# A Winograd-style 3x3 convolution on one core: a fourth image pair loaded in fp32, later casting loads in halves, fixed output buffers

## The chip, the core and the metric

The kernel runs on one core of a Trainium2 chip. The metric is the device time of one execution in microseconds (us). The core has the engines PE (matrix multiply, TensorE), PEld (its weight loads), DVE (VectorE), ACT (ScalarE), POOL (GpSimd) and SP (SyncE, which here only issues transfers). Transfers between the main memory and the on-chip memory run on 16 DMA engines. Three engines issue them, each through a queue of its own: SP (q1 in the profile), ACT (q10) and POOL (q0). Only POOL's transfers change the data type on the way ("casting loads").

## The reference

`x` is 16 images of 64 channels by 64 x 64 (fp32), `weight` is 128 x 64 x 3 x 3, and the output is 16 x 128 x 64 x 64 in fp32:

```
x_pad = np.pad(x, ((0, 0), (0, 0), (1, 1), (1, 1)))
output[b, co] += weight[co, ci, kh, kw] * x_pad[b, ci, kh:kh+h, kw:kw+w]
```

## The kernel before

The 16 images are taken as 8 pairs, p = 0 to 7. The two images of a pair stand in the two halves of the 128 partitions, 64 channels each. One pair is 2.1 MB in fp32 and gives two output tiles (one per image) of 2.1 MB each.

The kernel works on two output rows at once. With G0, G1, G2 for the three kernel rows, the sum of two neighbouring input rows (`ss`) goes through G1 once, and the even and the odd output row get a correction each, through the weight combinations G2 - G1 and G0 (even) and G0 - G1 and G2 (odd). `xs` is a pair in fp16, `ss` the sums of its row pairs in fp16.

A pair has four blocks (`blk`) of eight row pairs. A block runs three groups of matmuls (L174), each with one accumulator per image: U from `ss`, A and Bt from `xs`. ACT copies U out of the accumulators (L188), DVE adds it to A (L196) and to Bt (L199) and so writes the two output tiles `ots`. A block takes PE about 3.2 us, a pair about 12.8.

How the input comes (lines 40 to 64, 103 to 120, 134 to 140):

- Pairs 0, 1 and 2 come in fp32 by SP's queue, one transfer each, issued at the start (L43, L45, L47), into three of the seven output buffers. They are cast to `xs` on the chip: pair 0 by ACT and POOL, pairs 1 and 2 by ACT between its copies (the table `later`, L115 to L120).
- Pairs 3 to 7 come by POOL's casting loads (`load`, L56 to L64) straight into `xs`. Pairs 3 and 4 are issued in the setup, whole (L113). Pairs 5, 6 and 7 are issued in pair 1, after the row sums of pair 2 (L138 to L140): pair 5 whole, 6 and 7 in two halves of 32 rows.
- POOL makes the row sums of pair p+1 at the head of pair p, in two halves (L137), in program order with the loads that it issues.

How the output goes: image 0 of a pair is stored by SP, image 1 by ACT one block later (the list `held`). Pair 0 stores image 0 in halves, pair 7 both images, all others whole.

Buffers: `opool` has seven buffers of 128 x 16 KB under one tag, used in rotation: x0, x1, x2, then the output tiles of pair 0 and so on. Eight `xs` buffers hold all eight pairs, so no casting load waits for one. `keep` fixes the written order of an instruction on its engine.

Of the kernel before, what the change touches and what calls it, by code (L numbers as in the profile page):

```python
# [8 lines left out]
F32 = mybir.dt.float32  # L9
F16 = mybir.dt.float16  # L10
# [3 lines left out]
def kernel(  # L14
# [6 lines left out]
    nc = tc.nc  # L21
    B, CI, H, W = x.shape
    CO = weight.shape[0]
    assert H == 64 and W == 64 and CI == 64 and CO == 128 and B % 2 == 0
    NP = B // 2
# [3 lines left out]
    x_rows = x.rearrange("b c h w -> (b c) h w")  # L29
# [3 lines left out]
    const = ctx.enter_context(tc.tile_pool(name="const", bufs=1))  # L33
    psum = ctx.enter_context(tc.tile_pool(name="psum", bufs=8, space=bass.MemoryType.PSUM))
    xpool = ctx.enter_context(tc.tile_pool(name="xpool", bufs=8))
    opool = ctx.enter_context(tc.tile_pool(name="opool", bufs=7))
    spool = ctx.enter_context(tc.tile_pool(name="spool", bufs=3))
    upool = ctx.enter_context(tc.tile_pool(name="upool", bufs=4))

    w_raw = const.tile([CO, CI * 9], F32)  # L40
    nc.sync.dma_start(w_raw, w_flat)
    x0 = opool.tile([128, H, W], F32, tag="ot", name="x0")
    nc.sync.dma_start(x0, x_rows[0:128, :, :])  # L43
    x1 = opool.tile([128, H, W], F32, tag="ot", name="x1")
    nc.sync.dma_start(x1, x_rows[128:256, :, :])  # L45
    x2 = opool.tile([128, H, W], F32, tag="ot", name="x2")
    nc.sync.dma_start(x2, x_rows[256:384, :, :])  # L47
    raws = {1: x1, 2: x2}
    ident = const.tile([128, 128], F16)
    make_identity(nc, ident)  # L50
    w16 = const.tile([CO, CI * 9], F16)
    keep(nc.gpsimd.tensor_copy(w16, w_raw))  # L52

    xs = {p: xpool.tile([128, H, W], F16, tag="xs", name="xs") for p in range(3)}

    def load(p, rows):  # L56
        xs[p] = xpool.tile([128, H, W], F16, tag="xs", name="xs")
        for lo in range(0, H, rows):
            keep(
                nc.gpsimd.dma_start(  # L60
                    xs[p][:, lo : lo + rows, :],
                    x_rows[128 * p : 128 * p + 128, lo : lo + rows, :],
                )
            )  # L64
# [3 lines left out]
    def sums(eng, p, src, lo, n):  # L68
        if p not in ss:
            ss[p] = spool.tile([128, H // 2, W], F16, tag="ss", name="ss")  # L70
        v = src.rearrange("p (j i) c -> p j i c", i=2)
        keep(
            eng.tensor_add(  # L73
                ss[p][:, lo : lo + n, :], v[:, lo : lo + n, 0, :], v[:, lo : lo + n, 1, :]
            )
        )
# [26 lines left out]
    def cast(copy, p, src, lo, hi):  # L103
        keep(copy(xs[p][:, lo:hi, :], src[:, lo:hi, :]))  # L104
# [5 lines left out]
    keep(nc.scalar.copy(wrow(G2), wps[2]))  # L110
    cast(nc.gpsimd.tensor_copy, 0, x0, 34, 50)
    cast(nc.gpsimd.tensor_copy, 0, x0, 50, 64)
    for p in (3, 4):  # L113
        load(p, H)
    later = {  # L115
        (0, 0): [(0, x0, 18, 34)],
        (0, 2): [(1, x1, 0, 16), (1, x1, 16, 32)],
        (0, 3): [(1, x1, 32, 48), (1, x1, 48, 64)],
    }
    later.update({(1, n): [(2, x2, 16 * n, 16 * n + 16)] for n in range(4)})  # L120

    held = []

# [4 lines left out]
    def store(eng, p, b2, ot, lo, hi):  # L128
        return eng.dma_start(
            out_rows[2 * p + b2, :, lo:hi, :],  # L130
            ot.rearrange("p j i c -> p (j i) c")[:, lo:hi, :],
        )

    for p in range(NP):
        if p + 1 < NP:
            for lo in (0, 16):
                sums(nc.gpsimd, p + 1, raws.get(p + 1, xs[p + 1]), lo, 16)  # L137
                if (p, lo) == (1, 16):  # L138
                    for q in range(5, NP):
                        load(q, H if q == 5 else H // 2)  # L140
        ots = [
            opool.tile([128, H // 2, 2, W], F32, tag="ot", name="ot") for _ in range(2)
        ]
        for blk in range(4):
            j0 = blk * RB

            def group(wi_rows):

                tiles = [
                    psum.tile([128, RB, W], F32, tag="acc", name="acc") for _ in range(2)  # L150
                ]
                n = 3 * len(wi_rows)
                i = 0
                for wi, off in wi_rows:
                    for kw in (1, 0, 2):
                        c_lo, c_hi = max(0, 1 - kw), min(W, W + 1 - kw)
                        for b2 in range(2):
                            p0 = 64 * b2
                            lo, hi = j0, j0 + RB
                            if off is None:  # L160
                                rhs = ss[p][p0 : p0 + 64, lo:hi, c_lo + kw - 1 : c_hi + kw - 1]
                            else:
                                while 2 * lo + off < 0:
                                    lo += 1
                                while 2 * (hi - 1) + off > H - 1:
                                    hi -= 1
                                first = 2 * lo + off
                                last = 2 * (hi - 1) + off
                                rhs = xs[p][
                                    p0 : p0 + 64,  # L170
                                    first : last + 1 : 2,
                                    c_lo + kw - 1 : c_hi + kw - 1,
                                ]
                            nc.tensor.matmul(  # L174
                                tiles[b2][:, lo - j0 : hi - j0, c_lo:c_hi],
                                Wt[p0 : p0 + 64, wi, kw, :],
                                rhs,
                                start=i == 0,
                                stop=i == n - 1,
                            )  # L180
                        i += 1
                return tiles

            U = group([(G1, None)])
            us = []
            for b2 in range(2):
                ut = upool.tile([128, RB, W], F32, tag="ut", name="ut")
                keep(nc.scalar.copy(ut, U[b2]))  # L188
                us.append(ut)
            while held and (p, blk) != (1, 0):  # L190
                keep(store(nc.scalar, *held.pop(0)))
            for piece in later.get((p, blk), ()):
                cast(nc.scalar.copy, *piece)
            A = group([(G21, 1), (G0, -1)])
            for b2 in range(2):
                nc.vector.tensor_add(ots[b2][:, j0 : j0 + RB, 0, :], A[b2], us[b2])  # L196
            Bt = group([(G01, 0), (G2, 2)])
            for b2 in range(2):
                nc.vector.tensor_add(ots[b2][:, j0 : j0 + RB, 1, :], Bt[b2], us[b2])  # L199
            if blk in cuts_of[p][0]:  # L200
                store(nc.sync, p, 0, ots[0], *cuts_of[p][0][blk])
            if blk in cuts_of[p][1]:
                held.append((p, 1, ots[1], *cuts_of[p][1][blk]))
# [32 lines left out]
```

## Time and profile before

| | |
|---|---|
| median of 3 runs | 126.4 us (126.16 to 126.71) |
| the profiled execution | 126.62 us; span 124.8 us |
| PE busy | 108.0 us, without a gap from 9.7 to 112.3 us |
| DMA moved | 45.52 MB as the packets count it; HBM read 17.07 MB, written 33.55 MB |
| DMA queues, share of 16 engines' span | SP 45.0%, ACT 31.7%, POOL 20.8% |

The span runs from the first to the last instruction. The slices of the page cut it in 40 equal parts, each with the busy share in tenths. A DMA queue's share is the time of its packets over 16 engines' time. A casting load's MB are those that it writes (fp16), half of those that it reads.

### The profile page before, as it was taken

The page shows a single profiled execution, that of the slowest core. Times are in us where ns is not written, and L with a number is a line of the kernel's source. Part 1 is how long each engine was busy: PE and PEld are TensorE (multiplying, and loading weights), DVE is VectorE, ACT ScalarE, POOL GpSimd, SP SyncE. Part 2 cuts the span into 40 slices and gives each one's busy share as a digit, 9 for nine tenths or more (in the row PEclk, how much of TensorE's full clock was granted, in tenths as well). Part 3 has the DMA queues.
Part 4 walks back from the last instruction along what each step waited for, and adds up shares of the span by engine and source line. Part 5 has one row for each costly group of instructions (what it writes and reads, how often), then busy time and mean ns, then how long its engine had stood idle before and what let it go on. Part 6 is the DMA issues. An engine that isn't in the chain of part 4 may idle for free.

```text
span 124.8 us, 2430 instructions
## 1 busy us (share of the span) xinstructions
PE 108.0 (86%) x984; PEld 49.8 (40%) x984; DVE 84.5 (68%) x135; ACT 46.5 (37%) x78; POOL 38.6 (31%) x30
## 2 busy tenths in 40 slices
PE   0699999999999999999999999999999999990000
PEld 0544444444444444444444444444444444430000
DVE  1019987877777887888777778777877787774000
ACT  4118559966653333333333333333333333330000
POOL 2219780799975001910240032004200510000000
PEclk9999999999999999999999999999999999999555
DMA  5899999999999999999999999999999999999991
GB/s 163 367 430 451 430 302 247 278 276 312 365 344 333 341 370 385 382 392 375 370 381 386 382 400 369 354 406 400 374 369 404 425 420 430 420 420 430 428 404 68
DMA packets 4330, 45.52 MB, mean 365 GB/s; under 512 B 480, under 2 KB 480, under 8 KB 1120
## 3 DMA queue, kind: packets, MB, share of 16 engines
q1 hardware_dynamic: 2016, 23.36, 45.0%
q10 hardware_dynamic: 1296, 16.78, 31.7%
q0 software_dynamic: 1008, 5.24, 20.8%
q8 instruction: 7, 0.11, 0.3%
q14 instruction: 3, 0.02, 0.0%
HBM read 17.07 MB, written 33.55 MB: 406 GB/s over the span
## 4 chain that ended last, share of the span: by engine, by line
PE 86%; DMA 2%; DVE 1%; issue 1%; POOL 1%; DVEq 0%
PE acc L174 81%; PE warm L97 3%; DMA w_raw<-in_weight_dram 2%; PE wp L91 1%; DVE ot L196 1%; POOL w L52 1%; DVEq L231 0%; DVE ot L199 0%; DVEq L196 0%
## 5 line engine op out<-in xcount | busy, mean ns | idle before, releaser
L174 PE MATMUL acc<-xs,Wt 64*128 64x504 f16 (+3 forms) x768 | 87.0, 374 | 0.0
L174 PEld LDWEIGHTS <-Wt 64*128 64x128 f16 x960 | 46.9, 95 | 56.2 <-issue 0.9
L188 ACT COPY ut<-acc 128x512 f32<-128x512 f32 x64 | 34.4, 589 | 56.9 <-issue 39.0
L196 DVE TENSOR_TENSOR ot<-acc,ut 128x512 f32<-128x512 f32 x64 | 41.2, 685 | 20.8 <-PE acc L174 18.4
L199 DVE TENSOR_TENSOR ot<-acc,ut 128x512 f32<-128x512 f32 x64 | 41.1, 683 | 0.0
L73 POOL TENSOR_TENSOR ss<-xs 128x1024 f16<-128x1024 f16 x10 | 21.1, 2130 | 49.3 <-DMA xs<-in_x_dram 49.3
L174 PE MATMUL acc<-ss,Wt 64*128 64x504 f16 (+1 forms) x192 | 26.0, 377 | 0.0
L104 ACT CAST xs<-x 128x1024 f16<-128x1024 f32 (+1 forms) x10 | 10.5, 1070 | 3.3 <-DMA x<-in_x_dram 3.3
L73 POOL TENSOR_TENSOR ss<-x 128x1024 f16<-128x1024 f32 x4 | 9.4, 2358 | 5.0 <-DMA x<-in_x_dram 5.0
L73 DVE TENSOR_TENSOR ss<-x 128x512 f16<-128x512 f32 x4 | 3.3, 868 | 7.5 <-DMA x<-in_x_dram 7.5
L91 PE MATMUL wp<-ident,w 128*64 128x128 f16 x18 | 1.3, 328 | 4.3 <-POOL w L52 4.3
L104 POOL CAST xs<-x 128x1024 f16<-128x1024 f32 (+1 forms) x2 | 3.0, 1518 | 4.5 <-DMA x<-in_x_dram 4.5
L97 PE MATMUL warm<-blank 128*128 128x400 f32 x6 | 4.2, 864 | 0.0
L60 POOL DMA_DIRECT2D xs<-in_x_dram x7 | 3.9, 574 | 0.0
L91 PEld LDWEIGHTS <-w 128*64 128x64 f16 x18 | 1.1, 210 | 4.3 <-POOL w L52 4.3
L97 PEld LDWEIGHTS warm<-blank 128*128 128x128 f32 x6 | 1.8, 326 | 1.4 <-issue 1.3
L98 ACT CAST Wt<-wp 128x384 f16<-128x384 f32 x1 | 0.5, 478 | 3.0 <-PE wp L91 3.0
L98 ACT ACT_TABLE_LOAD x1 | 1.3, 1283 | 0.7 <-PEq L220 0.7
L52 POOL CAST w<-w_raw 128x576 f16<-128x576 f32 x1 | 0.7, 663 | 2.3 <-DMA w_raw<-in_weight_dram 2.3
L94 DVE MEMSET blank<- 128x400 f32 x1 | 0.4, 392 | 0.9 <-PEq L220 0.9
L109 ACT CAST Wt<-wp 128x384 f16<-128x384 f32 x1 | 0.5, 478 | 0.5 <-DVE Wt L101 0.5
L100 DVE TENSOR_TENSOR Wt<-wp,Wt 128x384 f16<-128x384 f32 x1 | 0.6, 551 | 0.0
(8 smaller groups left out, 1.9 us busy)
## 6 DMA issues: line engine op xcount, KB each, us to landing
out_dram<-ot ACTq DMA_DIRECT2D x7, 2048.0 KB, 19.0
out_dram<-ot SPq DMA_DIRECT2D x6, 2048.0 KB, 18.3
x<-in_x_dram SPq DMA_DIRECT2D x3, 2048.0 KB, 12.0
out_dram<-ot SPq DMA_DIRECT2D x4, 1024.0 KB, 12.6
xs<-in_x_dram POOLq DMA_DIRECT2D x3, 1024.0 KB, 22.0
xs<-in_x_dram POOLq DMA_DIRECT2D x4, 512.0 KB, 51.2
out_dram<-ot ACTq DMA_DIRECT2D x2, 1024.0 KB, 11.1
w_raw<-in_weight_dram SPq DMA_DIRECT2D x1, 288.0 KB, 2.8
```

The lines of the kernel that those rows point to most:

```text
L52: keep(nc.gpsimd.tensor_copy(w16, w_raw))
L60: nc.gpsimd.dma_start(xs[p][:, lo : lo + rows, :], x_rows[128 * p : 128 * p + 128, lo : lo + rows, :],)
L73: eng.tensor_add(ss[p][:, lo : lo + n, :], v[:, lo : lo + n, 0, :], v[:, lo : lo + n, 1, :])
L91: nc.tensor.matmul(wp[q : q + 64, k * CO : k * CO + CO], w16[:, t::9], ident)
L97: nc.tensor.matmul(warm[:, 0:400], blank[:, 0:128], blank)
L98: keep(nc.scalar.copy(wrow(G1), wps[1]))
L100: keep(nc.vector.tensor_sub(wrow(G21), wps[2], wrow(G1)))
L104: keep(copy(xs[p][:, lo:hi, :], src[:, lo:hi, :]))
L174: nc.tensor.matmul(tiles[b2][:, lo - j0 : hi - j0, c_lo:c_hi], Wt[p0 : p0 + 64, wi, kw, :], rhs, start=i == 0, stop=i == n - 1,)
L188: keep(nc.scalar.copy(ut, U[b2]))
L196: nc.vector.tensor_add(ots[b2][:, j0 : j0 + RB, 0, :], A[b2], us[b2])
L199: nc.vector.tensor_add(ots[b2][:, j0 : j0 + RB, 1, :], Bt[b2], us[b2])
```

## The change

Pair 3 is loaded like pairs 0 to 2: in fp32 by SP's queue at the start, into an output buffer, and cast to fp16 by ACT, in four pieces during pair 2's blocks. Its row sums are made by POOL from the fp32 data.

Pair 4 stays one whole casting load, but POOL issues it in pair 0, after the row sums of pair 1, instead of in the setup. Pairs 5, 6 and 7 are issued in pair 1, after the row sums of pair 2, as before, and all three now in halves.

The seven buffers become seven tags of one buffer each (`home0` to `home6`). x0 to x3 take homes 0 to 3; the output tiles follow a written list, `out_home`.

```diff
-    opool = ctx.enter_context(tc.tile_pool(name="opool", bufs=7))
+    opool = ctx.enter_context(tc.tile_pool(name="opool", bufs=1))
...
-    x0 = opool.tile([128, H, W], F32, tag="ot", name="x0")
-    nc.sync.dma_start(x0, x_rows[0:128, :, :])
-    x1 = opool.tile([128, H, W], F32, tag="ot", name="x1")
-    nc.sync.dma_start(x1, x_rows[128:256, :, :])
-    x2 = opool.tile([128, H, W], F32, tag="ot", name="x2")
-    nc.sync.dma_start(x2, x_rows[256:384, :, :])
-    raws = {1: x1, 2: x2}
+    HEAD = 4
+    out_home = [(4, 5), (6, 0), (1, 2), (3, 4), (5, 6), (0, 1), (2, 3), (4, 5)]
+    raws = {}
+    for p in range(HEAD):
+        raws[p] = opool.tile([128, H, W], F32, tag=f"home{p}", name="raw")
+        nc.sync.dma_start(raws[p], x_rows[128 * p : 128 * p + 128, :, :])
+    x0, x1 = raws[0], raws[1]
...
-    xs = {p: xpool.tile([128, H, W], F16, tag="xs", name="xs") for p in range(3)}
+    xs = {p: xpool.tile([128, H, W], F16, tag="xs", name="xs") for p in range(HEAD)}
...
-    for p in (3, 4):
-        load(p, H)
...
-    later.update({(1, n): [(2, x2, 16 * n, 16 * n + 16)] for n in range(4)})
+    for p in (2, 3):
+        later.update({(p - 1, n): [(p, raws[p], 16 * n, 16 * n + 16)] for n in range(4)})
...
-                if (p, lo) == (1, 16):
-                    for q in range(5, NP):
-                        load(q, H if q == 5 else H // 2)
+                if lo == 16 and p < 2:
+                    for q in ((4,), range(5, NP))[p]:
+                        load(q, H if q < 5 else H // 2)
         ots = [
-            opool.tile([128, H // 2, 2, W], F32, tag="ot", name="ot") for _ in range(2)
+            opool.tile([128, H // 2, 2, W], F32, tag=f"home{k}", name="ot")
+            for k in out_home[p]
         ]
```

## The prediction

> **What bounds the kernel now.** I read the page first (busy shares, slices, chain), then the stretches, then the DMA queues stretch by stretch, and last what POOL waited for.
>
> ```profile
> PE 108.0 (86%) x984; PEld 49.8 (40%) x984; DVE 84.5 (68%) x135; ACT 46.5 (37%) x78; POOL 38.6 (31%) x30
> ...
> PE   0699999999999999999999999999999999990000
> ...
> DMA  5899999999999999999999999999999999999991
> ...
> PE acc L174 81%; PE warm L97 3%; DMA w_raw<-in_weight_dram 2%; PE wp L91 1%; DVE ot L196 1%; POOL w L52 1%; DVEq L231 0%; DVE ot L199 0%; DVEq L196 0%
> ```
>
> The chain names PE, and PE has no gap from 9.7 to 112.3 us. But the slices show four empty ones for PE at the end, while DMA stays full until the last. Two things run without a pause: PE to 112.3, and the 16 DMA engines from about 2 us to the end. Only the second reaches the end. The stretches give its size (after the clock come the DMA share and GB/s):
>
> ```profile
> 5.00:10.00 5.00, 5.00 (x22) 2.50 (x20) 1.23 (x3) 1.61 (x2) 1.20 (x1) 1.00 1.01 433
> ...
> 20.00:25.00 5.00, 5.00 (x50) 2.33 (x48) 3.68 (x7) 4.59 (x7) 2.37 (x2) 1.00 0.99 251
> ...
> 110.00:115.00 5.00, 2.30 (x23) 0.88 (x18) 2.94 (x5) 0.95 (x2) 0.00 (x0) 1.00 0.95 403
> 115.00:120.00 5.00, 0.00 (x0) 0.00 (x0) 0.00 (x0) 0.00 (x0) 0.00 (x0) 0.52 1.00 424
> 120.00:124.80 4.80, 0.00 (x0) 0.00 (x0) 0.00 (x0) 0.00 (x0) 0.00 (x0) 0.50 0.45 189
> ```
>
> The share is 0.95 to 1.04 in every stretch from 5 to 120 us. The low 251 GB/s at 20 us is no lull: a casting load is counted by the fp16 it writes, half of what it reads. An average DMA engine is done at 120 + 0.45 x 4.8 = 122.2; the last one and its landing make it 124.8. So the time is the DMA engines' total work, plus how unevenly it falls on them. When the last SP store is issued (113.1), (115 - 113.1) x 0.95 + 5.0 + 2.2 = 9.0 us of DMA work is left. The last two half stores, 2.1 MB at 424 GB/s, are 4.9 of it; 4.1 us are older backlog. A PE that ends a little later would not be seen.
>
> The price of one piece (one partition's row of a transfer) by queue, over 4 to 12, 13 to 25, 26 to 34 and 64 to 98 us in this order:
>
> ```profile
> q1 hardware_dynamic: 225, 3.42, 100.2%
> ...
> q1 hardware_dynamic: 225, 2.63, 52.3%
> q0 software_dynamic: 152, 1.12, 49.3%
> ...
> q0 software_dynamic: 113, 0.82, 48.8%
> ...
> q0 software_dynamic: 389, 1.40, 20.3%
> ```
>
> Share x 16 engines x length, divided by the pieces (MB over 16,384 bytes in fp32, 8,192 in fp16, 4,096 for halves): fp32 alone 128.3 / 209 = 0.615 us; fp32 beside casts 100.4 / 160.5 = 0.626; casts from 13 to 25 us 94.7 / 137 = 0.691; casts from 26 to 34 us 62.5 / 100 = 0.624; half-size casts 110.4 / 342 = 0.323.
>
> **The change part by part.** A pair is 128 pieces, 8 on each DMA engine.
>
> Pair 3 in fp32 instead of cast. HBM reads stay 2.1 MB. At best it takes 8 x (0.691 - 0.615) = 0.61 us out of each DMA engine's work, if the slow casts of 13 to 25 us go with it; at worst, 8 x (0.626 - 0.624) = 0.02 is added. I take -0.4: pair 3 is the load that ran in that slow stretch, but pair 4 will start in a similar crowd, beside the last of x3 and the first stores.
>
> Pair 5 in halves: 16 x 0.323 - 8 x 0.624 = +0.18 at most, 0 if what each queue loses is covered by the other two. I take +0.1.
>
> SP issues one more load: 0.43 us (the three issues took 0.42 to 0.43). SP then waits until 17.1 for its first store, so it costs nothing. That store, in SP's queue, now stands behind x3. x1 landed at 13.7 and a fp32 pair alone takes 8 x 0.615 = 4.9 us, so x2 and x3 land near 18.5 and 23.5. The store moves by some 5 us; its buffer is next written by pair 3's output, after 48 us.
>
> POOL issues seven casting loads as before (0.56 us each), now one whole and six halves. Loads 3 and 4 left the slot at 11.7, where POOL was waiting for x1 anyway (0.75 us idle left); load 4 now follows the sums of pair 1, so it is issued at 13.7 + 4.7 = 18.4. x2 lands before POOL asks, so the 4.23 us wait for x2 goes; the sums of pair 2 run 19.0 to 23.7, six issues of 0.56 end near 27.1 (they ended at 29.9). DMA has work throughout: x3 until 23.5, load 4, both half stores of pair 0 (17.1, 23.7), and ACT's store at 26.7.
>
> POOL's sums of pair 3 read fp32: 2 x (2.36 - 2.12) = 0.5 us more, covered by 49.3 us of waiting for casting loads. ACT casts x3 in four pieces of 1.06 us during pair 2. In pair 1 the same four pieces stood between the same copies and PE did not pause; ACT's idle of 2.1 us per block in pair 2 takes them. Cost 0; if that cover were gone, 1.06 us of PE per block, 4.2 in all.
>
> The homes: each output tile still follows the same predecessor three to four pairs back. New meetings are x3 with pair 3 and x2 with pair 2's second tile; ACT's last cast of pair 1 ended at 35.0, and pair 2's first output, one block of 3.2 us after the last of pair 1, came at 37.5. Cost 0; without that cover DVE waits for one cast, 1.06 us.
>
> What is late next is the last casting half. POOL's waits show the landings, and the next line what PE does with them:
>
> ```profile
> 34.99 4.21 POOL L73 TENSOR_TENSOR ss<-xs 128x1024 f16<-128x1024 f16 x2 [0.82 <-DMA xs<-in_x_dram]
> 49.40 4.21 POOL L73 TENSOR_TENSOR ss<-xs 128x1024 f16<-128x1024 f16 x2 [10.20 <-DMA xs<-in_x_dram]
> 61.66 2.12 POOL L73 TENSOR_TENSOR ss<-xs 128x1024 f16<-128x1024 f16 x1 [8.06 <-DMA xs<-in_x_dram]
> 73.69 2.12 POOL L73 TENSOR_TENSOR ss<-xs 128x1024 f16<-128x1024 f16 x1 [9.91 <-DMA xs<-in_x_dram]
> 86.04 2.13 POOL L73 TENSOR_TENSOR ss<-xs 128x1024 f16<-128x1024 f16 x1 [10.23 <-DMA xs<-in_x_dram]
> 98.21 2.12 POOL L73 TENSOR_TENSOR ss<-xs 128x1024 f16<-128x1024 f16 x1 [10.04 <-DMA xs<-in_x_dram]
> ...
> 105.73 0.81 PE L174 MATMUL acc<-ss,Wt 64*128 64x512 f16 x6
> ```
>
> Whole pair 5 took 14.4 us after pair 4; then each half took 12.2, about one pair of stores. The soonest landing of a whole cast was 13.8 us after its issue, so pair 4 lands near 32.2. Pair 5's two halves then take 14.4 (by bytes) to 24.4 (by turns), and four more 48.8: the last half lands between 95.4 and 105.4. POOL adds 2.1, and PE wants that sum at 105.7: the limit is 103.6. The later end would stop PE for 1.8 us, and the backlog of 4.1 us, less the start of a store (2.1 us: the 0.295 MB of weights landed after 2.82, of which 0.7 are moving), hides at least 2.0. So 0. By the Trainium skill, DMA: Bandwidth & Descriptors, Queues, rings and completion order, each DMA engine takes the queues in turn a packet at a time; by that rule the later end is the right one, and the sum stays.
>
> Sum: 126.62 (the profiled execution, span 124.8) - 0.4 + 0.1 = 126.3. It lies 0.2 above the median of the runs, so against 126.4 the forecast is **126.1**.
>
> **The rivals.**
> A, faster: the whole slow stretch goes. From 13 to 25 us 2.63 + 2 x 1.12 = 4.87 MB were read or written, 406 GB/s against 428 alone: 0.6 us lost; together with 2.6 us between the average engine's end and the last, of which a third may go when one cast load less disturbs single engines, -0.6 to -1.5: 124.9 to 125.8, say 125.4. For it: only casts were slow there. Against: seven casting loads remain in number.
>
> B, slower: PE starves for pair 7's second half. If six halves advance at the pace of the stores, 12.8 us a pair (102.6 us of PE over 8), the last lands at 32.2 + 6 x 12.8 = 109.0, PE stops 5.4 us, 2 to 4.1 are hidden: +1.3 to +3.4, near 128.5. It decides from a landing at 105.6 on. Against: where stores ran out, the cast queue went faster.
>
> C, slower: one transfer more costs its fixed time, 2.1 us by the weights' row, because nothing runs beside it: 128.5. The DMA share of 0.95 to 1.04 across all borders between transfers speaks against it. The Trainium skill, DMA: Bandwidth & Descriptors, Anatomy of one DMA, gives about 2.0 us for each transfer; by that alone the time would be 128.4 (an estimate), and the trace shows the cost covered.
>
> D, slower: the uneven ends of the engines grow by a third, +0.9: 127.3. Nothing speaks for it but that the order changes.
>
> **How the numbers follow.** A measurement of this kernel tells about 0.5% (0.63 us) from no change. My case, 125.8 to 127.0, has 0.50; A 0.30; B 0.12; D 0.05; C 0.03. Faster is A, same my case, slower B, C and D: 0.20. The range for 8 in 10 goes from 125.2 (most of A) to 127.3 (D), leaving out B and C and some of A. The likeliest case's own range is 125.8 to 126.6: its two terms at their ends, -0.61 and +0.20.
>
> **What would show it.** PE still without a gap to 112.3; DMA share at 1 to 120 us and an average end near 121.9; fewer MB on q0 (4.2 instead of 5.24) and 25.5 MB on q1; casts in the first 25 us at 0.62 instead of 0.69; POOL's wait for x2 gone; its last wait ending between 100 and 105. I am wrong if PE idles for xs or ss in pair 7, if DMA pauses between 18 and 28 us, or if the last engine's end moves away from the average.

## The result, and the profile after

The changed kernel takes 126.73 us (median of 22 runs) against 126.17 for the kernel before: the ratio is 1.0042, with a 95% interval of 1.0030 to 1.0054. That is 0.56 us slower. The time lies in the forecast range and inside my middle case (125.8 to 127.0), but outside that case's own range (125.8 to 126.6), and the step has the other sign: I had put it 0.3 us below the kernel before. The profiled execution of the changed kernel took 127.35 us with a span of 125.6. It is the slowest of the 22, and the one before (126.62) is slower than its median too, so single traces are compared with care below.

From the page of the changed kernel, the DMA slices and the queues (packets, MB, share of 16 engines):

```profile
DMA  5999999999999999999999999999999999999980
...
q1 hardware_dynamic: 2160, 25.46, 48.8%
q10 hardware_dynamic: 1296, 16.78, 31.5%
q0 software_dynamic: 1008, 4.19, 16.8%
```

The stretches of the changed kernel:

```profile
15.00:20.00 5.00, 5.00 (x50) 2.24 (x48) 4.01 (x7) 2.79 (x5) 4.98 (x4) 1.00 0.99 423
20.00:25.00 5.00, 5.00 (x52) 2.28 (x50) 3.92 (x7) 4.53 (x8) 5.00 (x5) 1.00 1.03 329
...
110.00:115.00 5.00, 2.92 (x28) 1.15 (x24) 3.57 (x6) 1.07 (x2) 0.00 (x0) 1.00 0.98 413
115.00:120.00 5.00, 0.00 (x0) 0.00 (x0) 0.00 (x0) 0.00 (x0) 0.00 (x0) 0.65 1.01 426
120.00:125.60 5.60, 0.00 (x0) 0.00 (x0) 0.00 (x0) 0.00 (x0) 0.00 (x0) 0.50 0.41 174
```

The bytes moved from queue to queue as meant: 2.10 MB more on q1, 1.05 less on q0. PE is still busy in every stretch up to its end, and the DMA share is 0.98 or more from 15 to 120 us. The average DMA engine ends at 120 + 0.41 x 5.6 = 122.3, against 122.2 before, while the span is 0.8 us longer: nothing was gained in work, and in this trace the last engine ends further behind the average (3.3 us with its landing, 2.6 before). Added up, the three queues' shares times the span are 97.5% x 124.8 = 121.7 us per engine before and 97.1% x 125.6 = 122.0 after.

The tail of the DMA work from 119 to 126 us, in 40 slices of 0.175 us, before and then after:

```profile
GB/s 468 328 562 281 468 515 374 468 328 562 281 515 421 375 234 234 281 140 234 187 140 0 94 47 0 0 0 0 0 0 0 0 0 0 0 0 0 0 0 0
```

```profile
GB/s 421 421 421 374 421 515 421 421 421 421 374 421 468 468 281 281 234 187 234 281 187 94 0 47 0 47 47 0 47 0 0 0 0 0 0 0 0 0 0 0
```

47 GB/s over a slice is one piece of 8 KB. After the change a few single pieces trail, the last in the slice that ends at 124.1 us; before, the last is in the slice that ends at 123.2. One engine alone would leave such a tail, in this trace.

POOL in order of time in the changed kernel, then PE where it takes up the last row sums:

```profile
18.43 0.70 POOL L62 DMA_DIRECT2D xs<-in_x_dram  x1
19.15 4.70 POOL L75 TENSOR_TENSOR ss<-raw 128x1024 f16<-128x1024 f32 x2
23.79 3.22 POOL L62 DMA_DIRECT2D xs<-in_x_dram  x6
...
91.63 2.13 POOL L75 TENSOR_TENSOR ss<-xs 128x1024 f16<-128x1024 f16 x1 [10.22 <-DMA xs<-in_x_dram]
102.15 2.13 POOL L75 TENSOR_TENSOR ss<-xs 128x1024 f16<-128x1024 f16 x1 [8.39 <-DMA xs<-in_x_dram]
...
106.36 0.81 PE L176 MATMUL acc<-ss,Wt 64*128 64x512 f16 x6
```

POOL does what the forecast said, to within 0.2 us: load 4 at 18.4, no wait for x2, the six issues until 27.0. The last half lands at 102.15, inside the 95.4 to 105.4 given, and its row sums are ready 2.1 us before PE wants them. Rival B did not happen in this trace.

The price of a cast near 22 us is where the forecast broke. The casting queue from 20 to 26 us, first before and then after:

```profile
q0 software_dynamic: 110, 0.77, 68.6%
```

```profile
q0 software_dynamic: 59, 0.48, 43.8%
```

Share x 6 us x 16, over MB / 8,192 bytes: 65.9 / 94 = 0.70 us for a piece before, 42.0 / 59 = 0.72 after. The slow casts did not go with pair 3. Pair 4 now stands in that stretch and pays the same in this kernel.

### The profile page after: what moved, and what is told of

It reads as the page before. It is cut to its first block, busy times and chain, and to the rows that moved or that the text cites. A ratio compares the mean times of both kernels' runs of the same rounds, so it can differ in the third digit from the quotient of the medians.

```text
span 125.6 us, 2436 instructions
## 1 busy us (share of the span) xinstructions
PE 108.5 (86%) x984; PEld 49.0 (39%) x984; DVE 84.7 (67%) x135; ACT 50.4 (40%) x82; POOL 39.2 (31%) x30
## 3 DMA queue, kind: packets, MB, share of 16 engines
q1 hardware_dynamic: 2160, 25.46, 48.8%
## 4 chain that ended last, share of the span: by engine, by line
PE 85%; DMA 2%; DVE 1%; issue 1%; POOL 1%; DVEq 0%
PE acc L176 81%; PE warm L99 3%; DMA w_raw<-in_weight_dram 2%; PE wp L93 1%; DVE ot L198 1%; POOL w L54 1%; DVE ot L201 0%; DVEq L233 0%; DVEq L198 0%
## 5 line engine op out<-in xcount | busy, mean ns | idle before, releaser
L176 PEld LDWEIGHTS <-Wt 64*128 64x128 f16 x960 | 46.1, 94 | 57.5 <-issue 1.4
L75 POOL TENSOR_TENSOR ss<-xs 128x1024 f16<-128x1024 f16 x8 | 17.0, 2127 | 55.6 <-DMA xs<-in_x_dram 45.0
L106 ACT CAST xs<-raw 128x1024 f16<-128x1024 f32 (+1 forms) x14 | 14.7, 1067 | 3.3 <-DMA raw<-in_x_dram 3.3
L75 POOL TENSOR_TENSOR ss<-raw 128x1024 f16<-128x1024 f32 x6 | 14.1, 2383 | 1.9 <-DMA raw<-in_x_dram 1.9
L75 DVE TENSOR_TENSOR ss<-raw 128x512 f16<-128x512 f32 x4 | 3.3, 868 | 7.6 <-DMA raw<-in_x_dram 7.6
L106 POOL CAST xs<-raw 128x1024 f16<-128x1024 f32 (+1 forms) x2 | 3.0, 1521 | 4.5 <-DMA raw<-in_x_dram 4.5
```

The costliest lines, as they stand in the source:

```text
L75: eng.tensor_add(ss[p][:, lo : lo + n, :], v[:, lo : lo + n, 0, :], v[:, lo : lo + n, 1, :])
L176: nc.tensor.matmul(tiles[b2][:, lo - j0 : hi - j0, c_lo:c_hi], Wt[p0 : p0 + 64, wi, kw, :], rhs, start=i == 0, stop=i == n - 1,)
```

## The experiments

All ratios are against the kernel before, timed on the same chip, with 95% intervals. "Work" is the three queues' shares times the span, as above, good to about 0.1 us; it is that of the one profiled execution. The expectations name four theories: S, a single DMA engine that falls behind in x3 sets the end; L, PE's later end does; H, the halves cost DMA work; T, a late end of the casting queue costs.

**Both kernels once more.** No edit.

> The changed kernel once more, for a second trace of it. Theory S (a straggling DMA engine): the mean work of the DMA engines is as before the change, but one engine falls 2 to 3 us behind in x3 between 19 and 24 us and stays behind; expected again: ratio 1.003 to 1.006, the slowest fp32 load lands 23.5 us or more after its issue, and single pieces trail after 123.5 us. Rival L (late PE): the end follows PE's end, 0.6 us later in the first trace (last SP store issued at 113.7 instead of 113.1); then the two issue times differ again by the same 0.6 us. Rival H (halves): pieces of 4 KB cost, 0.2 us on every DMA engine; then no straggler is needed.

> The kernel before once more, for a second trace of it, and for the spread between two samples of one program: ratio 1.000 within 0.002. Theory S: the last landings are spread over several engines again, without one alone at the end. Rival L: the last SP store is issued at 113.1 within 0.2 us again; if it is at 113.7 here too, the 0.6 us are no property of the change.

Measured: 1.0058 (1.0032 to 1.0084) and 0.998 (0.9949 to 1.0011). The slowdown is real and of the same size. The last SP store was issued at 114.3 in the second trace of the kernel before, later than in both traces of the changed one (113.7). That trace is unusual: x0 landed 1.1 us late, and the time (127.75) is the longest of its sample. But 113.7 is also seen in the kernel before with load 4 late (below), which costs nothing, so PE's later end is no property of the change (rival L falls). The last stretch, kernel before and then changed kernel, second traces:

```profile
120.00:125.90 5.90, 0.00 (x0) 0.00 (x0) 0.00 (x0) 0.00 (x0) 0.00 (x0) 0.50 0.42 178
```

```profile
120.00:125.90 5.90, 0.00 (x0) 0.00 (x0) 0.00 (x0) 0.00 (x0) 0.00 (x0) 0.50 0.41 172
```

The average DMA engine ends at 122.5 and 122.4, and the spans are 125.9 and 124.8. So now it is the kernel before whose last engine is 3.4 us behind, and the changed one's 2.4. The trailing engine of the first trace is no property of the change (theory S is not borne out), and two traces of one program differ by more than the effect.

**PE later.** Two more warm-up products in the kernel before.

```diff
-    for _ in range(3):
+    for _ in range(5):
         nc.tensor.matmul(warm[:, 0:400], blank[:, 0:128], blank)
```

> The kernel before, with five warm-up products instead of three, so that PE and all that follows it starts 2.7 to 2.8 us later; nothing of the computation is changed. If the DMA engines' work is the bound and 4 us of older stores are waiting at PE's end: ratio 1.000 to 1.006, with the last SP store issued near 115.9. If PE's end sets the time, as the chain says: 1.021.

Measured: 1.0019 (1.0000 to 1.0037). The two added products took 1.05 us (the warm-up 5.21 us instead of 4.16) and the warm-up began 0.24 us later, so PE was late by 1.3 us, not 2.7. Last SP store and the stretches behind it:

```profile
114.38 0.33 SPq L129 DMA_DIRECT2D out_dram<-ot  x1
```

```profile
115.00:120.00 5.00, 0.00 (x0) 0.00 (x0) 0.00 (x0) 0.00 (x0) 0.00 (x0) 0.83 1.01 423
120.00:124.50 4.50, 0.00 (x0) 0.00 (x0) 0.00 (x0) 0.00 (x0) 0.00 (x0) 0.50 0.55 231
```

The store was issued 1.3 us later than before (113.1), and the time rose by 0.2% (0.24 us; the interval reaches to none). If PE's end set the time, 1.3 us would have been a ratio of 1.010. Most of PE's lateness is hidden by older stores: the DMA engines, not the chain's PE, set the end.

**Load 4's moment.** The change undone, and then done alone.

```diff
+    load(4, H)          # changed kernel, before the table of later casts
...
-                if lo == 16 and p < 2:
-                    for q in ((4,), range(5, NP))[p]:
+                if (p, lo) == (1, 16):
+                    for q in range(5, NP):
```

> The changed kernel with load 4 issued in the setup, where load 3 was before, so that x2 and x3 come beside a casting load. Theory S: the engine that fetches instructions near 19 us then does it amid two queues, as before the change, and no single engine is 2.6 us late on x3: ratio 0.998 to 1.001. Rival L: PE's end as in the changed kernel, 1.004. Rival H: the six halves are still there, so 1.003 to 1.005.

Measured: 1.0052 (1.0023 to 1.0081). Theory S fails in the number it gave. The casting queue from 20 to 26 us in this run, with pair 4's load in the place of pair 3's:

```profile
q0 software_dynamic: 80, 0.53, 42.6%
```

That is 40.9 / 64.7 = 0.63 us for a piece: here the casts are not slow. But SP's queue has more work, 49.5% x 125.1 = 61.9 us against 48.8% x 125.6 = 61.3 in the changed kernel, and POOL's has 0.6 less, so the work is 122.0 in both. The dear pieces moved to another queue and the sum stayed.

Rival B is also seen in this trace: the last half landed at 104.0, past my limit of 103.6, and PE's next sum product started 2.83 us after the products before it (2.60 in the changed kernel's second trace), a pause of 0.2 us:

```profile
104.00 2.12 POOL L75 TENSOR_TENSOR ss<-xs 128x1024 f16<-128x1024 f16 x1 [10.05 <-DMA xs<-in_x_dram]
```

```profile
103.34 2.76 PE L177 MATMUL acc<-xs,Wt 64*128 64x512 f16 x24
106.17 0.83 PE L177 MATMUL acc<-ss,Wt 64*128 64x512 f16 x6
```

```diff
-    for p in (3, 4):
-        load(p, H)
+    load(3, H)          # kernel before
...
-                if (p, lo) == (1, 16):
-                    for q in range(5, NP):
-                        load(q, H if q == 5 else H // 2)
+                if lo == 16 and p < 2:
+                    for q in ((4,), range(5, NP))[p]:
+                        load(q, H if q < 6 else H // 2)
```

> The kernel before, with load 4 issued in pair 0 after the row sums of pair 1; pair 3 still a casting load in the setup, pair 5 whole. If the moment of load 4 does the harm (its casts then run from 22 to 30 us beside the first stores), ratio 1.002 to 1.004. If it is the fp32 load of pair 3 with an engine falling behind in x3, 1.000. The last casting half lands 0 to 2 us later than before; PE does not wait.

Measured: 0.9996 (0.9976 to 1.0017). The moment of load 4 costs nothing in the kernel before (the last SP store was issued at 113.7 in this trace).

**Pair 5 whole in the changed kernel** (fp32 for pair 3 and the late load 4 remain).

```diff
-                        load(q, H if q < 5 else H // 2)
+                        load(q, H if q < 6 else H // 2)
```

> The changed kernel with pair 5 as one whole casting load. Rival H: the 0.2 us of the halves go, and so ratio 1.001 to 1.003. Theory S: x3 and the moment near 19 us are untouched, so 1.003 to 1.006, and the slowest fp32 load is again about 23.5 us from issue to landing. Rival L: 1.004.

Measured: 1.0038 (1.0012 to 1.0065), and once more, below, 1.0030 (1.0015 to 1.0045). So the change without the halves of pair 5 costs 0.3 to 0.4%, where I had a gain of 0.4 us for pair 3. The late load 4 costs nothing when it is alone; that leaves fp32 for pair 3, with ACT's casts and the fixed buffers that go with it, by subtraction only. The work (121.5 and 121.8 in the two traces) is no more than that of the kernel before.

**Pair 5 in halves alone**, in the kernel before.

```diff
-                        load(q, H if q == 5 else H // 2)
+                        load(q, H // 2)
```

> The kernel before, with pair 5 in halves and nothing else. Theory H (halves cost): the half-size pieces add 0.2 to 0.3 us of work to each DMA engine, as between the changed kernel and the one with pair 5 whole; ratio 1.0015 to 1.003. Theory S (only the straggler in x3 counts): 1.000.

Measured: 1.0062 (1.0036 to 1.0089). So the halves alone cost as much as the whole change, and more than the work that is added in this trace: 97.6% x 125.2 = 122.2 against 121.7 and 121.9 in the two traces before, 0.3 to 0.5 us, where the time rose by 0.8. The last half landed at 102.9, against 98.2 before.

**No halves at all**, in the kernel before and in the changed one.

```diff
-                        load(q, H if q == 5 else H // 2)   # kernel before
+                        load(q, H)
...
-                        load(q, H if q < 5 else H // 2)    # changed kernel
+                        load(q, H)
```

> The kernel before, with pairs 6 and 7 as whole casting loads too. Theory H: two pairs less in halves take 0.3 to 0.6 us from each DMA engine's work; ratio 0.995 to 0.9975, and this beats both kernels. By turns the whole loads land near 49, 63 and 78 us, well ahead of PE. Theory S: 1.000.

> The changed kernel with pairs 4 to 7 all as whole casting loads. Theory T: the casting queue ends near 75 us, so ratio 0.999 to 1.002. Theory H: 0.4 to 0.6 us less of work than in the changed kernel, ratio 0.999 to 1.002 too. Theory S (a DMA engine that falls behind in x3 decides): 1.003 to 1.006, x3 being untouched.

Measured: 1.0022 (0.9997 to 1.0047) and 1.0042 (1.0030 to 1.0054). The queues of the kernel before with all pairs whole:

```profile
q1 hardware_dynamic: 2016, 23.36, 45.1%
q10 hardware_dynamic: 1296, 16.78, 31.8%
q0 software_dynamic: 720, 5.24, 20.5%
```

That is 97.4% x 124.5 = 121.3 us of work, 0.4 to 0.6 less than before, and no gain in time. In the changed kernel the work fell to 121.5 and the time stayed where it was. Theory H holds for the work and fails for the time.

**Where the halves stand.** Three pairs in halves, but the early ones; and load 7 later with no more pieces.

```diff
-        load(p, H)                          # pairs 3 and 4
+        load(p, H // 2)
...
-                        load(q, H if q == 5 else H // 2)
+                        load(q, H // 2 if q == 5 else H)
```

> The kernel before, with pairs 3, 4 and 5 in halves and 6 and 7 whole: three pairs of half-size pieces, as many as in the changed kernel and in the kernel before with pair 5 in halves, but the casting queue is through sooner, near 85 to 92 us instead of 102 to 103. Theory T (the late end of the casting queue costs): ratio 0.999 to 1.002. Theory H (the pieces themselves cost, wherever they are): 1.003 to 1.006.

```diff
-                if (p, lo) == (1, 16):
-                    for q in range(5, NP):
+                if lo == 16 and p in (1, 5):
+                    for q in {1: (5, 6), 5: (7,)}[p]:
```

> The kernel before, with load 7 issued in pair 5, after the row sums of pair 6, and not in pair 1; no piece more or less. The casting queue stands empty for some 4 us near 76 us and ends near 102 to 104 instead of 98. Theory T: ratio 1.003 to 1.006. Theory H: 1.000, unless DMA engines stand idle meanwhile, which the DMA share from 75 to 85 us would show.

Measured: 1.0026 (1.0013 to 1.0038) and 1.0035 (1.0011 to 1.0059). In the second the DMA engines were not idle while the casting queue stood empty, and the last half came at 103.75:

```profile
75.00:80.00 5.00, 5.00 (x52) 2.32 (x48) 3.69 (x7) 1.80 (x4) 1.89 (x3) 1.00 1.00 426
```

```profile
75.78 1.10 POOL L60 DMA_DIRECT2D xs<-in_x_dram  x2
92.83 2.12 POOL L73 TENSOR_TENSOR ss<-xs 128x1024 f16<-128x1024 f16 x1 [15.95 <-DMA xs<-in_x_dram]
103.75 2.13 POOL L73 TENSOR_TENSOR ss<-xs 128x1024 f16<-128x1024 f16 x1 [8.80 <-DMA xs<-in_x_dram]
```

Issuing load 7 late thus costs 0.35% with no piece more, as theory T said (1.003 to 1.006). That the late end of the queue is the reason is not shown: the profiled execution took 125.96 us, no more than the kernel before, and had the late end all the same. With the halves early the casting queue was through near 91.7 us, and they still cost 0.26%, a little more than T allowed and less than H; the work there, three pairs in halves, is 97.9% x 124.4 = 121.8, no more than before.

**x3 by ACT's queue**, issued between 10.5 and 11.0 us in the traces: with pair 5 whole, with pair 5 in halves (the changed kernel in all else), and with all pairs whole; beside them x3 by SP and pair 5 whole again.

```diff
-        nc.sync.dma_start(raws[p], x_rows[128 * p : 128 * p + 128, :, :])
+        if p < 3:
+            nc.sync.dma_start(raws[p], x_rows[128 * p : 128 * p + 128, :, :])
...
     keep(nc.scalar.copy(wrow(G2), wps[2]))
+    keep(nc.scalar.dma_start(raws[3], x_rows[384:512, :, :]))
```

> The changed kernel with pair 5 whole and with x3 loaded by ACT's queue instead of SP's, issued after the two weight copies near 11.5 us; x2 and x3 then come side by side, and x3 no longer stands ahead of SP's first stores. Theory S (x3 in SP's queue ahead of the first stores lets one DMA engine fall behind, and that sets the end): no DMA engine 2.5 us late in SP's first stores, ratio 0.999 to 1.002. If fp32 for pair 3 costs by itself, in whatever queue it comes: 1.003 to 1.005, as with x3 by SP.

> The changed kernel in all else, with x3 by ACT's queue, issued near 11.5 us. If x3's place in SP's queue, ahead of the first stores, makes the changed kernel slower: 0.999 to 1.002. If the halves of pair 5 do (some 0.25 us of DMA work for a halved pair): 1.003 to 1.006.

> x3 by ACT's queue and pairs 4 to 7 all whole: the least DMA work of all variants, by the sums of the queues' shares some 0.5 us less than with two pairs halved. If the work sets the time: 0.996 to 0.999, faster than both kernels. If the uneven ends of the DMA engines outweigh such terms, as with all pairs whole before: 1.000 to 1.003.

> The changed kernel with pair 5 whole and x3 by SP, once more, on one chip with the two others, for the comparison of the queues: 1.002 to 1.005 if x3 by SP costs and x3 by ACT does not; equal to x3 by ACT within 0.0015 if the first difference between them was chance.

Measured, in this order: 1.0013 (0.9994 to 1.0032), 1.0093 (1.0057 to 1.0129), 1.0020 (0.9996 to 1.0043) and 1.0030 (1.0015 to 1.0045). The second against the first is the halving of pair 5 alone, and the intervals are apart: 0.8%; the second has only five executions in its interval and was timed on another chip than the first, each against the kernel before on its own chip. Its last half landed at 99.9, and the first's at 98.2, so a late end of the casting queue does not explain this 0.8%. x3's place in SP's queue does not explain the changed kernel, since without it the time is no better; and x3 by ACT against x3 by SP, with pair 5 whole, is 0.0017, with intervals that overlap. The third has the least work of all:

```profile
q1 hardware_dynamic: 2016, 23.36, 45.0%
q10 hardware_dynamic: 1440, 18.88, 36.1%
q0 software_dynamic: 576, 4.19, 16.2%
```

97.3% x 124.4 = 121.0 us, 0.7 less than before, and not faster. No variant beats the kernel before.

## Why the prediction was wrong, and where it was right

What bounds the kernel: right. PE ends 12 us before the end, the DMA share stays near 1, and a PE that was 1.3 us later cost 0.2%. The page's chain, which gives PE 86% of the span, would have had 1.3 us. POOL's new order, the buffers and ACT's four casts make no engine wait, as said: PE has no pause in the changed kernel's two traces. The forecast's list of new meetings in the buffers left one out, x0 with the second tile of pair 1 (home 0); DVE, which writes that tile, waits for no cast in the trace.

"Pair 3 in fp32 instead of cast ... I take -0.4": this step failed. The forecast charged the slow casts (0.691 us a piece) to pair 3 and gave them back with it. They were not pair 3's own: from 20 to 26 us a cast cost 0.70 us with pair 3 there and 0.72 with pair 4, and when pair 4 was issued early the casts took 0.63 but SP's queue 0.6 us more. The sentence of the forecast that pair 4 "will start in a similar crowd" should have led to the other end of the range, +0.02. In work, the change with pair 5 whole is at 121.5 and 121.8 us against 121.7 and 121.9: a gain of 0.1 or so, where -0.4 was forecast. In time, the same kernel costs 0.3 to 0.4% (0.4 to 0.5 us) in two runs, outside the forecast's range for this term altogether.

"Pair 5 in halves ... I take +0.1, at most +0.18": this step failed too. The price of a piece was right (0.323 before; after, from 64 to 98 us, 22.7% of 34 us x 16 over 381 pieces is 0.324). But the time rose by 0.8 us where pair 5 was halved alone in the kernel before, and by 1.0 with x3 on ACT's queue; the work in those traces rose by 0.3 to 0.5, and with three early pairs in halves by 0.1 at most. So neither the price of the pieces nor the work accounts for it, and the later end of the casting queue is no sure reason either. In the changed kernel with x3 by SP the same halving is worth at most 0.3% (1.0042 and 1.0058 against 1.0038 and 1.0030, with intervals that overlap): the two parts of the change do not add up, and which term was the more wrong depends on what stands beside it.

Rival D (uneven ends, +0.9, chance 0.05) is the nearest of the four to what the first trace shows: the average engine ends 0.1 us later, the last one 0.8. The second pair of traces shows the opposite, so D is not borne out; that its 127.3 us is near the first trace's 127.35 is luck. The forecast's own sign of being wrong, a last engine that moves away from the average, showed in the first trace alone. Rival A fell with the slow casts. In rival B's question the last half came at 102.2 and 102.9 us, nearer to the count by turns (105.4) than to that by bytes (95.4); in the two variants where it passed the limit (104.0 and 103.75) PE paused for 0.2 and 0.1 us, less than the backlog of 4.1 us. Rival C did not happen: the DMA share is 0.98 or more across the borders between transfers.

What stays open is why the time does not follow the work. Taking 0.2 to 0.9 us of work away (three variants without halves) gained nothing, adding 0.3 to 0.5 cost 0.8 to 1.0. The end is that of the last of 16 engines. The kept traces hold 16 landings for each transfer, as many as there are DMA engines, and the last store's say more than the mean. In the first traces the last landing but one is at 123.5 us in both kernels, and the last at 123.9 before and 124.7 after. In the second traces the last but one is at 123.7 in both, and the last at 125.0 in the kernel before and 123.9 in the changed one; in all four the span ends 0.9 to 1.0 us later. So one late landing makes most of the difference between two traces of a program (0.8 to 1.1 us), it comes and goes in both kernels, and it does not explain the change: the changed kernel's second trace has none, and at 126.58 us it is still slower than the median of the kernel before, 126.1. The two traces of the kernel before are themselves slower than that median, so they do not show how its usual execution ends. What makes the usual execution of the changed kernel half a microsecond longer is not shown.

## What to carry to other kernels

When a transfer looks slow in one stretch, ask whether it is the transfer itself that is slow before crediting its removal: the next load in that place, or the queue beside it, may pay the same. Where the DMA engines are full from start to end, a step priced in their average work is only half of the answer, because the last engine ends the kernel; the sign of a forecast of a few tenths of a microsecond then rests on little. Before a trailing engine in one trace is given as a cause, take a second trace of both kernels: here it changed sides. Cutting a load in two is not free beside busy queues: in the kernel before it moved the last landing 4.7 us later (98.2 to 102.9) and cost 0.6%, though a piece cost little more than its bytes (0.323 us for a half, 0.624 for a whole).

## What I had not expected of the hardware

A casting load beside two busy store queues advances more by pieces than by bytes: halves landed 10.5 to 12.3 us apart in the changed kernel (79.29, 91.63, 102.15) and 12.0 to 12.4 before, whole loads of twice the bytes, with as many pieces, 14.4. In both kernels a cast piece took 0.70 to 0.72 us between 20 and 26 us, against 0.62 later in the kernel before, whichever pair's load stood there; with pair 4 issued early it took 0.63 in the same stretch, and SP's queue 0.6 us more in all. The cause was not found.
